# Key norms of a pair at once, spread by way of DRAM, in a hybrid RWKV-7 and dilated-attention layer

## The chip, the cores and the metric

One core of one Trainium2 chip. The metric is device time in microseconds of one execution; several executions give a median. The engines are TensorE (PE for products, PEld for its weight loads), VectorE (DVE), ScalarE (ACT), GpSimd (POOL) and SyncE (SP, which issues most DMAs).

## The reference

One layer of a decoder with two branches that run over the same projected input: RWKV-7 time mixing (8 heads of 64) and dilated attention (3 groups of 4 heads of 128). There are 1024 prompt tokens and 32 sample tokens (8 sequences of 4). The change lies in time mixing; what it computes there:

```python
h = x @ w_in                                   # (T, 9344): r | k | v | lora | gates | q | k | v | ...
zs_mixed = zs + mu_shift * (prev - zs)         # token shift of the first 1664 columns
w = -softplus(-(w0 + tanh(wd) @ w_w2)) - 0.5;  decay = exp(-exp(w))
a = sigmoid(a0 + ad @ w_a2)
kk = (k * k_k).reshape(B, T, R_HEADS, R_HD)
kk = kk / maximum(norm(kk, axis=-1), 1e-12)    # one norm for each token and head
k = k * (1.0 + (a - 1.0) * k_a)
# scan over tokens, per head:
#   sa = S @ (-kk_t);  S = S * w_t + sa (kk_t * a_t)^T + v_t k_t^T;  o_t = S @ r_t
```

then a group norm of o, a bonus term, a gate; the attention; and x <- LayerNorm(ALPHA x + W_out(g_r * (Y_r W_oa) + g_a * (Y_a W_ob))).

## The kernel before

The tokens run along the free dimension and the columns of the projections along the 128 partitions, so a column tile of 128 holds two heads of time mixing: a *pair*. A projection of one column tile (`project_steps`) is 72 products, in two halves of the contraction and three stretches of 352 tokens, into three banks of the tag `pj` (four in all). Its weights come in halves through `wraw` (two buffers) and are split into `whi` and `wlo` (three buffers each).

The time-mixing stage runs five streams against each other:

- `products`: for each of the four pairs the projections of k, r and v (`pair_tiles`, which keeps them shifted in tiles `m` of 1024 tokens, four buffers), and 24 projections that nothing in this stage needs soon (`fill`: gates), whose results go through tiles `zt` to DRAM. The projection of a pair's k may begin at once, those of r and v once `done["prep"] >= 2 * j`.
- `units`: eight preparations (`unit`), one for each pair j and half hf of 512 tokens. A unit squares the keys, sums the squares over each head's rows with a product against `bones` (lines 317 to 320), takes the inverse root in a chain of small DVE operations (`rsqrt`, lines 150 to 155), widens it to 64 columns a head (line 327), turns that back with four transposes (line 343), so that kkn, the normed keys, can be formed (line 345). Beside it go the low-rank products (line 301) and the decay. BK and KR are then multiplied in line 378, which gives AT. KR and what follows wait until the scan of the unit two places before is done.
- `inverses`: a triangular inverse on DVE for each unit. AT's blocks go by DRAM (Yd, then Y), lines 449 and 452 work on X, and X goes back by DRAM (Xd, line 456; AT from Xd, line 470), then T1 (line 471).
- `scans`: for each unit four rounds of small products (from line 476; lines 484 and 494 use T1), then eight hops, each two products (lines 535 and 541) with DVE and ACT between (lines 536, 537, 544).
- `norms`: group norm, gate, and the store of the branch's output.

`units` ends with `sample_rows`, which prepares the sample tokens' vectors and stores them to DRAM (`vd`).

The order of TensorE's instructions is written out by hand: `run_streams` keeps a clock of its own. Each generator yields a pair, the time that its products take and the delay after which it may go on (constants such as D_KR = 1.81, D_AT = 4.5, D_UP = 8.4 and D_ST, in us); between them pieces of `products` are put. A stream that yields None waits for a condition. The other engines' order comes from the scheduler below the kernel. All instructions of an engine, and all DMA issues of a queue, run in their order. After this stage come attention with its own projections, the two branch products, and the output product (line 1421).

The tag `g` has two PSUM banks (norm sums, low-rank products, transposes and others), `sc` two (scans).

Of the kernel before, what the change touches and what calls it, by code (L numbers as in the profile page):

```python
# [14 lines left out]
AF = mybir.ActivationFunctionType  # L15
ALU = mybir.AluOpType
AX = mybir.AxisListType

P = 128
D = 1024  # L20
KT = D // P
SEQ = 1024
NB = 8
NT = 4
NS = NB * NT
# [4 lines left out]

PIECE = 3
D_PN, D_KR, D_AT, D_G, D_W, D_INV, D_UP = 0.65, 1.81, 4.5, 0.2, 2.09, 1.3, 8.4
D_PM, D_HOP, D_ST, D_GN, D_IN, D_U0, D_MASK = 0.9, 1.25, 1.54, 12.6, 11.0, 1.2, 1.2
SMALL = 1.0
RS = 8
CDEC = math.exp(-0.5)
# [48 lines left out]
def tile_layer(ctx: ExitStack, tc: tile.TileContext, A: dict, O: list):  # L85
# [223 lines left out]
        return consume  # L309


    def unit(j, hf, Mr, Mk, Mv, st, out):
        sl = slice(512 * hf, 512 * hf + 512)
        t_ = lambda tag="t", n=6: mk(rp, [P, 512], tag, n)
        c2p = lambda a: a.rearrange("p (a b c) -> p a b c", a=4, b=2)
        sq = t_()
        S.activation(sq[:], Mk[:, sl], AF.Square, scale=prm[:, KK + j : KK + j + 1])
        pn = ps("g")
        for c2 in range(4):
            T.matmul(pn[:, 2 * c2 : 2 * c2 + 2], sq[:, c2 * P : (c2 + 1) * P], bones[:, 0:P:64], start=True, stop=True)  # L320
        yield (0.4, 0.6)
        nt = mk(rp, [P, 24], "nt", 1)
        n2, rn, tn = nt[:, 0:8], nt[:, 8:16], nt[:, 16:24]
        V.tensor_scalar(n2, pn[:, 0:8], 1e-24, None, ALU.max)
        rsqrt(rn, n2, tn)
        rb = t_()
        V.tensor_copy(rb.rearrange("p (a b) -> p a b", a=8), rn.unsqueeze(2).to_broadcast([P, 8, 64]))
        pw, pa = ps("g"), ps("g")
        lora(((pw[:], 0, j), (pa[:], 1, j)), sl)
        yield (1.3, D_PN)  # L330
# [6 lines left out]
        V.tensor_tensor_scan(lam[:], rmask, sg[:], 0.0, ALU.mult, ALU.add)  # L337
        Ei = t_()
        S.activation(Ei[:], lam[:], AF.Exp, scale=0.5 * CDEC)
        yield (0.0, D_KR)  # L340
        pn = ps("g")
        for c2 in range(4):
            T.transpose(pn[:, c2 * P : (c2 + 1) * P], rb[:, c2 * P : (c2 + 1) * P], ident)
        kkn = t_()
        V.scalar_tensor_tensor(kkn[:], Mk[:, sl], prm[:, KK + j : KK + j + 1], pn[:], ALU.mult, ALU.mult)
        bt = t_()
        V.scalar_tensor_tensor(bt[:], ta[:], 1.0, kkn[:], ALU.add, ALU.mult)
        f2 = t_()
# [3 lines left out]
        BK = mk(rp, [P, 4, 4, 64], "BK", 1)  # L352
        V.scalar_tensor_tensor(BK[:, :, 1:3, :], c2p(bt), 0.5, c2p(Ei), ALU.mult, ALU.mult)
        V.tensor_tensor(BK[:, :, 0:4:3, :], c2p(k2), c2p(Ei), ALU.mult)
        yield (0.45, 0.0)
        while done["scan"] < 2 * j + hf - 1:
            yield None
        E = mk(rp, [P, 8, 65], "E", 2)
        G.memset(E[:, :, 0:1], 1.0)
        S.activation(E[:, :, 1:65], lam.rearrange("p (a b) -> p a b", a=8), AF.Exp, scale=-0.5 * CDEC)  # L360
# [29 lines left out]
                )  # L390
            yield (0.9, D_MASK)
        masked.append((j, hf, AT))
        while done["norm"] < 2 * j + hf - 1:
            yield None
        bon = t_("bon", 2)
        pb = ps("g")
        T.matmul(pb[:], bones, rk[:], start=True, stop=True)
# [163 lines left out]
    def norm(j, hf, Ot, bon):  # L561
        sl = slice(512 * hf, 512 * hf + 512)
        t_ = lambda tag, n: mk(rp, [P, 512], tag, n)
        Og = Ot.rearrange("p a (b c) -> p (a b) c", b=2)
        m8 = mk(rp, [P, 8], "m8", 1)
        V.tensor_reduce(m8[:], Og, AX.X, ALU.add)
        V.tensor_scalar(m8[:], m8[:], 1.0 / 64.0, None, ALU.mult)
        V.tensor_tensor(Og, Og, m8.unsqueeze(2).to_broadcast([P, 8, 64]), ALU.subtract)
        sq = t_("sz", 2)
        S.activation(sq[:], Ot.rearrange("p a b -> p (a b)"), AF.Square)  # L570
        v8 = mk(rp, [P, 8], "v8", 1)
        V.tensor_reduce(v8[:], sq.rearrange("p (a b) -> p a b", a=8), AX.X, ALU.add)
        V.tensor_scalar(v8[:], v8[:], 1.0 / 64.0, GN_EPS, ALU.mult, ALU.add)
        nt = mk(rp, [P, 24], "nt", 1)
        r8 = nt[:, 0:8]
        rsqrt(r8, v8[:], nt[:, 8:16])
        V.tensor_tensor(Og, Og, r8.unsqueeze(2).to_broadcast([P, 8, 64]), ALU.mult)
        yield (0.0, D_GN)
        po = ps("g")
        for c2 in range(4):  # L580
            T.transpose(po[:, c2 * P : (c2 + 1) * P], Ot[:, c2, :], ident)
        y = Ot.rearrange("p a b -> p (a b)")
        S.activation(y, po[:], AF.Identity, scale=prm[:, LG + j : LG + j + 1], bias=prm[:, LB + j : LB + j + 1])
        V.tensor_tensor(y, y, bon[:], ALU.add)
        sz = t_("sz", 2)
        SP.dma_start(sz[:], zd[j, :, sl])
        V.tensor_tensor(y, y, sz[:], ALU.mult)
        SP.dma_start(yd[j, :, sl], y)
# [14 lines left out]
    pbc = lambda o: prm[:, o : o + 4].unsqueeze(2).to_broadcast([P, 4, NS])  # L603
    dbc = lambda o: der[:, o : o + 4].unsqueeze(2).to_broadcast([P, 4, NS])
    bns = mk(cpool, [P, 4, NS], "bns")
    vd = mk(dpool, [8, NS, 6, 64], "vd")


    def sample_rows():
        sgs, tas, nS, tS = (mk(rp, [P, 512], "t", 6)[:, 0:P].rearrange("p (a b) -> p a b", a=4) for _ in range(4))  # L610
        rS, kS_, vS_ = (sM[:, 4 * i : 4 * i + 4, :] for i in range(3))
        bs = [ps("g") for half in range(2)]
        for j in range(4):
            lora([(bs[half][:, NS * j : NS * j + NS], half, j) for half in range(2)], slice(SEQ, TOK))
        yield 0.6, D_G
        for b, dst, off in ((bs[0], sgs, HW0), (bs[1], tas, HA0)):
            for j in range(4):
                S.activation(dst[:, j, :], b[:, NS * j : NS * j + NS], AF.Tanh, scale=0.5, bias=der[:, off + j : off + j + 1])
        vec = mk(rp, [P, SEQ], "m", 4)[:, 0 : 24 * NS].rearrange("p (a b c) -> p a b c", a=6, b=4)

        V.tensor_scalar(sgs, sgs, 1.0, None, ALU.add)
        S.activation(vec[:, 0], sgs, AF.Exp, scale=-0.5 * CDEC)
        G.tensor_tensor(vec[:, 1], kS_, pbc(KK), ALU.mult)
        G.tensor_tensor(tS, vec[:, 1], vec[:, 1], ALU.mult)
        yield 0.0, 2.0
        b = ps("g")
        T.matmul(b[:, 0:P], bones, tS.rearrange("p a b -> p (a b)"), start=True, stop=True)
        nf = lambda a: a.rearrange("p a b -> p (a b)")
        V.tensor_scalar(nf(nS), b[:, 0:P], 1e-24, None, ALU.max)
        rS2 = mk(rp, [P, 512], "t", 6)  # L630
        rsqrt(rS2[:, 0:P], nf(nS), rS2[:, P : 2 * P])
        G.tensor_tensor(vec[:, 1], vec[:, 1], rS2[:, 0:P].rearrange("p (a b) -> p a b", a=4), ALU.mult)
        V.scalar_tensor_tensor(vec[:, 2], tas, 1.0, vec[:, 1], ALU.add, ALU.mult)
        V.tensor_scalar(vec[:, 2], vec[:, 2], 0.5, None, ALU.mult)
        G.tensor_tensor(vec[:, 3], tas, dbc(KAH), ALU.mult)
        G.tensor_tensor(vec[:, 3], vec[:, 3], dbc(KA2), ALU.add)
        G.tensor_tensor(vec[:, 3], vec[:, 3], kS_, ALU.mult)
        G.tensor_copy(vec[:, 4], rS)
        G.tensor_copy(vec[:, 5], vS_)
        G.tensor_tensor(tS, rS, vec[:, 3], ALU.mult)  # L640
        G.tensor_tensor(tS, tS, pbc(RK), ALU.mult)
        yield 0.2, 4.0
        b = ps("g")
        T.matmul(b[:, 0:P], bones, tS.rearrange("p a b -> p (a b)"), start=True, stop=True)
        V.tensor_tensor(bns[:], b[:, 0:P].rearrange("p (a b) -> p a b", a=4), vS_, ALU.mult)
        vt = mk(rp, [P, SEQ], "m", 4)[:, 0 : 6 * P].rearrange("p (a b) -> p a b", a=6)
        for h in range(2):
            yield 0.3, 1.0
            b = ps("g")
            for i in range(3):  # L650
                T.transpose(b[:, i * P : (i + 1) * P], vec[:, 3 * h + i].rearrange("p a b -> p (a b)"), ident)
            S.activation(vt[:, 3 * h : 3 * h + 3, :], b[:, 0 : 3 * P].rearrange("p (a b) -> p a b", a=3), AF.Copy)
        for hh in range(8):
            src = vt[NS * (hh // 2) : NS * (hh // 2) + NS, :, 64 * (hh % 2) : 64 * (hh % 2) + 64]
            SP.dma_start(vd[hh], src)

        yield 0.3, 1.0
        b = ps("g")
        T.transpose(b[0:117, 0:P], zl.rearrange("p a b -> p (a b)"), ident)
        zo = mk(rp, [P, P], "so", 1)  # L660
        V.tensor_copy(zo[0:117, :], b[0:117, 0:P])
        SP.dma_start(O[10][0, 0].rearrange("(a b) -> a b", b=P), zo[0:13, :])
        SP.dma_start(O[11][0].rearrange("s (a b) -> (s a) b", b=P), zo[13:117, :])
# [6 lines left out]
    def pair_tiles():  # L670
        for j in range(4):
# [2 lines left out]
                G.memset(t[:], 0.0)  # L674
            for c0, i, o in ((512, 1, 4), (0, 0, 0), (1024, 2, 8)):
                yield (lambda: True) if i == 1 else (lambda: done["prep"] >= 2 * j)
                M[i] = mk(rp, [P, SEQ], "m", 4)
                yield from project_steps(c0 + P * j, shifted(o + j, M[i]), PIECE)
            pairs[j] = M, st

    def products():
        pt = pair_tiles()
# [13 lines left out]
    def units():  # L696
        for u in range(8):
# [1 line left out]
            while j not in pairs:  # L699
                yield None  # L700
            M, st = pairs[j]
            yield from unit(j, hf, M[0], M[1], M[2], st, ready)
            done["unit"] += 1
        yield from sample_rows()

    def inverses():
# [760 lines left out]
```

## Time and profile before

| | us |
|---|---|
| median of 3 runs (lowest, highest) | 1369.14 (1366.88, 1371.59) |
| profiled execution, its time | 1371.35 |
| its span, first to last instruction | 1369.6 |
| busy: PE, PEld | 1331.2, 1241.9 |
| busy: DVE, ACT, POOL | 802.4, 469.4, 67.4 |
| mean granted TensorE clock | 0.993 |

All times in the rows are in us from the start of the span, unless marked ns. A row of a timeline has start, duration, engine, line, operation, what it writes and reads, how many instructions were merged (x), and in brackets how long the engine sat idle before it and what released it. A row of waits has who waited for whom, then total, times and longest. A row of a stretch has its length, then busy time and number of instructions of PE, PEld, DVE, ACT and POOL, the granted TensorE clock, the DMA engines' share and GB/s. A group's row has the count, then busy time and mean ns of one, then idle time before it. Rows of one line have minimum, median and maximum duration in ns, then first and last start. Matmuls are pipelined: a busy TensorE is not TensorE at its peak, and one instruction's duration is longer than the distance to the next. "PEq", "SPq" and the like are an engine's queue, which waits or issues.

### The profile page before, as it was taken

What the parts mean: (1) busy time and instruction counts of PE and PEld (TensorE: products, weight loads), DVE (VectorE), ACT (ScalarE), POOL (GpSimd) and SP (SyncE); (2) the same over time, 40 slices, a digit from 0 to 9 for tenths busy, and PEclk for the clock granted to TensorE, in tenths of its full rate; (3) what the DMA queues carried; (4) which work ended last, traced back from release to release, by engine and by line L of the source; (5) the groups of instructions that cost most, each with busy time, mean ns of one, the idle gap of its engine ahead of it and who ended that gap; (6) DMA issues with size and microseconds to landing.
All of it is one profiled execution on the core that took longest, in us unless ns stands there. A gap on an engine that the chain in (4) does not pass through costs nothing.

```text
span 1369.6 us, 25939 instructions
## 1 busy us (share of the span) xinstructions
PE 1331.2 (97%) x10097; PEld 1241.9 (91%) x10097; DVE 802.4 (59%) x2203; ACT 469.4 (34%) x1065; POOL 67.4 (5%) x82
## 2 busy tenths in 40 slices
PE   8999999999999999899999999999999998999997
PEld 7999899999998999899999999999999997899786
DVE  5467857685867757352554385437543744665565
ACT  5342434444444444332332323332332234132211
POOL 0000000000000000000000000000000000025100
PEclk9999999999999999899999999999999999999999
DMA  6123132313222232237555455555445666785221
GB/s 204 53 67 79 39 100 72 97 47 100 77 76 70 79 111 72 79 97 152 109 108 119 119 132 103 122 125 133 98 119 130 129 135 148 233 277 168 83 97 70
DMA packets 340271, 151.64 MB, mean 111 GB/s; under 512 B 188928, under 2 KB 329622, under 8 KB 339894
## 3 DMA queue, kind: packets, MB, share of 16 engines
q1 hardware_dynamic: 241270, 129.68, 34.4%
q10 hardware_dynamic: 98880, 20.32, 7.4%
q8 instruction: 79, 1.29, 0.4%
q14 instruction: 42, 0.34, 0.1%
HBM read 110.68 MB, written 38.97 MB: 109 GB/s over the span
## 4 chain that ended last, share of the span: by engine, by line
PE 81%; DVE 11%; DMA 4%; issue 2%; SPq 1%; ACT 1%; DVEq 0%; ACTq 0%
PE pj L173 59%; PE pj L1421 7%; PE o L975 2%; PE s L938 2%; DVE tm L449 2%; DVE X L452 2%; PE g L378 1%; PE t L958 1%; PE s L1057 1%; DMA cb<-cd 1%; DVE st L544 1%; PE sc L535 1%; DVE wlo L164 1%; PE sc L541 1%; PE g L552 1%
## 5 line engine op out<-in xcount | busy, mean ns | idle before, releaser
L173 PE MATMUL pj<-xhi,whi 128*128 128x352 f32 x1848 | 397.5, 336 | 4.6 <-ACT xhi L1288 3.0
L173 PE MATMUL pj<-xlo,whi 128*128 128x352 f32 x1848 | 384.2, 329 | 0.0
L173 PE MATMUL pj<-xhi,wlo 128*128 128x352 f32 x1848 | 383.6, 329 | 0.0
L173 PEld LDWEIGHTS pj<-xhi,whi 128*128 128x128 f32 x1848 | 304.9, 189 | 21.8 <-issue 11.4
L173 PEld LDWEIGHTS pj<-xlo,whi 128*128 128x128 f32 x1848 | 307.7, 190 | 2.7 <-issue 1.0
L173 PEld LDWEIGHTS pj<-xhi,wlo 128*128 128x128 f32 x1848 | 308.4, 190 | 1.8 <-issue 0.6
L164 DVE TENSOR_TENSOR wlo<-wraw,whi 128x512 fp32r<-128x512 f32 x162 | 113.1, 700 | 74.0 <-ACT whi L163 73.1
L163 ACT ACTIVATE whi<-wraw 128x512 fp32r<-128x512 f32 x162 | 100.5, 625 | 126.0 <-PE pj L173 80.8
L948 ACT ACTIVATE Sm<-Sm,nm 128x128 f32<-128x128 f32 (+1 forms) x96 | 42.4, 442 | 101.9 <-DVE nm L945 101.8
L449 DVE TENSOR_TENSOR tm<-Y,X 128x60 f32<-128x60 f32 (+24 forms) x248 | 52.7, 213 | 9.6 <-DMA Y<-Yd 3.7
L452 DVE TENSOR_TENSOR X<-X,tm 128x60 f32<-128x60 f32 (+24 forms) x248 | 52.3, 211 | 6.2
L940 DVE CUSTOM_DVE_ANT_0 Sm<-s,cst 128x128 f32<-128x128 f32 (+1 forms) x96 | 29.2, 346 | 40.6 <-PE s L938 40.0
L1421 PE MATMUL pj<-wl,mh 128*128 128x512 f32 (+1 forms) x136 | 52.0, 382 | 0.0
L544 DVE SCALAR_TENSOR_TENSOR st<-sc,E,SD 64x64 f32<-64x64 f32 x128 | 36.1, 282 | 22.8 <-PE sc L541 21.2
L533 ACT ACTIVATE SD<-st,E 128x128 f32<-128x128 f32 x64 | 25.6, 400 | 57.8 <-DVE st L544 57.7
L801 POOL TENSOR_TENSOR kvp<-vv,kv 128x512 f32<-128x512 f32 x16 | 19.7, 1234 | 498.0 <-DVE Ss L809 387.5
L975 PE MATMUL o<-PT,Vt 128*128 128x128 f32 x280 | 38.8, 276 | 0.8 <-ACT PT L962 0.8
L863 ACT ACTIVATE k<-pj 128x352 f32<-128x352 f32 (+1 forms) x36 | 16.2, 454 | 67.0 <-PE pj L173 62.7
L938 PE MATMUL s<-k,q 128*128 128x128 f32 (+1 forms) x192 | 37.7, 325 | 0.8 <-DVE ml L940 0.8
L975 PEld LDWEIGHTS o<-PT,Vt 128*128 128x128 f32 x280 | 36.4, 191 | 1.5 <-ACT PT L962 1.1
L536 DVE TENSOR_TENSOR W<-sc,R 64x128 f32<-64x128 f32 x64 | 18.4, 288 | 31.8 <-PE sc L535 30.7
L537 ACT ACTIVATE Ot<-sc 64x128 f32<-64x128 f32 x64 | 17.3, 270 | 57.5 <-DVE W L536 57.4
(320 smaller groups left out, 1706.7 us busy)
## 6 DMA issues: line engine op xcount, KB each, us to landing
wraw<-in_w_in_dram SPq DMA_DIRECT2D x146, 256.0 KB
gd<-zt SPq DMA_DIRECT2D x48, 176.0 KB
gt<-gd SPq DMA_DIRECT2D x48, 176.0 KB
vs<-bt ACTq DMA_DIRECT2D x48, 128.0 KB
kc<-in_cache_kv_g_dram SPq DMA_DIRECT2D x48, 128.0 KB
Vt<-vs ACTq DMA_DIRECT2D x12, 512.0 KB
cb<-cd SPq DMA_DIRECT2D x12, 512.0 KB
zd<-zt SPq DMA_DIRECT2D x24, 176.0 KB
```

What stands on the lines that cost most here:

```text
L163: S.activation(hi[:], raw[:], AF.Copy)
L164: V.tensor_tensor(lo[:], raw[:], hi.bitcast(F32)[:], ALU.subtract)
L173: T.matmul(out, w[wi][:, n % 4, :], x[:, n % 4, :], start=first and n == 0, stop=last and n == 11)
L449: V.tensor_tensor(tm, Y[:, r : r + 1, r + 1 : 32].to_broadcast([P, m, n]), X[:, 0:m, r : r + 1].to_broadcast([P, m, n]), ALU.mult)
L452: V.tensor_tensor(X[:, 0:m, r + 1 : 32], X[:, 0:m, r + 1 : 32], tm, ALU.subtract)
L533: S.activation(SD[:], S0[:], AF.Copy, scale=E[:, c, 64:65])
L544: V.scalar_tensor_tensor(S1[d, d], pS[d, d], E[d, c, 64:65], SD[d, d], ALU.mult, ALU.add)
L938: T.matmul(r, qT[:, i * P : (i + 1) * P], kT[:, keys[i][0] * P : keys[i][0] * P + n], start=True, stop=True)
L940: V.tensor_tensor_reduce(out=Sm[:, i, 0:n], in0=r, in1=m3 if g == 2 else m12[:, 256 - n : 256], scale=1.0, scalar=NEG, op0=ALU.add, op1=AL ...
L948: S.activation(Sm[:, i, 0:n], Sm[:, i, 0:n], AF.Exp, scale=SCALE, bias=nm[:, x : x + 1], accum_out=ml[:, g, 1, i : i + 1])
L975: T.matmul(po[:, (i % 4) * P : (i % 4 + 1) * P], st["Vt"][:, kb_, :], PT[:, n * P : (n + 1) * P], start=m == 0, stop=m == len(keys[i]) - 1,)
L1421: T.matmul(pb[:], a[:, k], wk, start=x == 0, stop=x == len(prods) - 1)
```

## The change

The norms of a pair are formed once, in its first unit (hf = 0), for both halves: two squares, eight products into 16 columns of one bank, one chain of small operations on 16 columns. The 128x16 result is stored to a DRAM tile `nd` [4, 2, 1024] in the order (pair, head of the pair, token). Each unit then loads its half, each head's row broadcast to the head's 64 partitions, into the tile `rb`, in the layout of the keys. The widening copy and the four transposes go. The delay ahead of kkn is doubled in first units, and the yield behind BK goes.

`pair_tiles` hands the pair over when its k is projected, and `unit` takes r and v out of the dictionary M where it needs them, waiting until they are there. `sample_rows` waits for seven scans, and stores `vd` with two DMAs in place of eight. D_ST is 1.65 in place of 1.54.

```diff
-D_PM, D_HOP, D_ST, D_GN, D_IN, D_U0, D_MASK = 0.9, 1.25, 1.54, 12.6, 11.0, 1.2, 1.2
+D_PM, D_HOP, D_ST, D_GN, D_IN, D_U0, D_MASK = 0.9, 1.25, 1.65, 12.6, 11.0, 1.2, 1.2
...
-    def unit(j, hf, Mr, Mk, Mv, st, out):
+    def unit(j, hf, M, st, out):
+        Mk = M[1]
...
-        sq = t_()
-        S.activation(sq[:], Mk[:, sl], AF.Square, scale=prm[:, KK + j : KK + j + 1])
-        pn = ps("g")
-        for c2 in range(4):
-            T.matmul(pn[:, 2 * c2 : 2 * c2 + 2], sq[:, c2 * P : (c2 + 1) * P], bones[:, 0:P:64], start=True, stop=True)
-        yield (0.4, 0.6)
-        nt = mk(rp, [P, 24], "nt", 1)
-        n2, rn, tn = nt[:, 0:8], nt[:, 8:16], nt[:, 16:24]
-        V.tensor_scalar(n2, pn[:, 0:8], 1e-24, None, ALU.max)
-        rsqrt(rn, n2, tn)
+
+        if hf == 0:
+            pn = ps("g")
+            for x in range(2):
+                sq = t_()
+                S.activation(sq[:], Mk[:, 512 * x : 512 * x + 512], AF.Square, scale=prm[:, KK + j : KK + j + 1])
+                for c2 in range(4):
+                    n = 4 * x + c2
+                    T.matmul(pn[:, n:16:8], sq[:, c2 * P : (c2 + 1) * P], bones[:, 0:P:64], start=True, stop=True)
+                yield (0.8, 0.6)
+            nt = mk(rp, [P, 48], "nt", 1)
+            n2, rn, tn = nt[:, 0:16], nt[:, 16:32], nt[:, 32:48]
+            V.tensor_scalar(n2, pn[:, 0:16], 1e-24, None, ALU.max)
+            rsqrt(rn, n2, tn)
+            SP.dma_start(nd[j].rearrange("e (c p) -> p (e c)", p=P), rn)
         rb = t_()
-        V.tensor_copy(rb.rearrange("p (a b) -> p a b", a=8), rn.unsqueeze(2).to_broadcast([P, 8, 64]))
+        for e in range(2):
+            SP.dma_start(rb[64 * e : 64 * e + 64, :], nd[j, e : e + 1, sl].to_broadcast([64, 512]))
         pw, pa = ps("g"), ps("g")
...
-        yield (0.0, D_KR)
-        pn = ps("g")
-        for c2 in range(4):
-            T.transpose(pn[:, c2 * P : (c2 + 1) * P], rb[:, c2 * P : (c2 + 1) * P], ident)
+        yield (0.0, D_KR if hf else 2.0 * D_KR)
         kkn = t_()
-        V.scalar_tensor_tensor(kkn[:], Mk[:, sl], prm[:, KK + j : KK + j + 1], pn[:], ALU.mult, ALU.mult)
+        V.scalar_tensor_tensor(kkn[:], Mk[:, sl], prm[:, KK + j : KK + j + 1], rb[:], ALU.mult, ALU.mult)
...
-        yield (0.45, 0.0)
-        while done["scan"] < 2 * j + hf - 1:
+        while done["scan"] < 2 * j + hf - 1 or 0 not in M:
             yield None
+        Mr = M[0]
...
-        while done["norm"] < 2 * j + hf - 1:
+        while done["norm"] < 2 * j + hf - 1 or 2 not in M:
             yield None
+        Mv = M[2]
...
-        for hh in range(8):
-            src = vt[NS * (hh // 2) : NS * (hh // 2) + NS, :, 64 * (hh % 2) : 64 * (hh % 2) + 64]
-            SP.dma_start(vd[hh], src)
+        for e in range(2):
+            SP.dma_start(vd.rearrange("(j e) s i c -> e j s i c", e=2)[e], vt[:, :, 64 * e : 64 * e + 64])
...
-                M[i] = mk(rp, [P, SEQ], "m", 4)
-                yield from project_steps(c0 + P * j, shifted(o + j, M[i]), PIECE)
-            pairs[j] = M, st
+                m = mk(rp, [P, SEQ], "m", 4)
+                yield from project_steps(c0 + P * j, shifted(o + j, m), PIECE)
+                M[i] = m
+                pairs[j] = M, st
...
-            yield from unit(j, hf, M[0], M[1], M[2], st, ready)
+            yield from unit(j, hf, M, st, ready)
             done["unit"] += 1
+        while done["scan"] < 7:
+            yield None
         yield from sample_rows()
```

The chain of small operations in the group norm takes its tile `nt` in the new size as well.

More of the change, by code (lines that the diff above doesn't have):

```diff
@@ L573, in norm @@
         V.tensor_scalar(v8[:], v8[:], 1.0 / 64.0, GN_EPS, ALU.mult, ALU.add)
-        nt = mk(rp, [P, 24], "nt", 1)
+        nt = mk(rp, [P, 48], "nt", 1)
         r8 = nt[:, 0:8]
@@ L605, in tile_layer @@
     bns = mk(cpool, [P, 4, NS], "bns")
+    nd = mk(dpool, [4, 2, SEQ], "nd")
     vd = mk(dpool, [8, NS, 6, 64], "vd")
```

## The prediction

> **What bounds the kernel now.** I read the page first, then the busy time by stretch, then TensorE's waits inside the stage that the change touches, and last the one place where these stand out. From the page: busy time, the slices, and the shares of the chain that ended last.
>
> ```profile
> PE 1331.2 (97%) x10097; PEld 1241.9 (91%) x10097; DVE 802.4 (59%) x2203; ACT 469.4 (34%) x1065; POOL 67.4 (5%) x82
> ...
> PE   8999999999999999899999999999999998999997
> ...
> PEclk9999999999999999899999999999999999999999
> ...
> PE 81%; DVE 11%; DMA 4%; issue 2%; SPq 1%; ACT 1%; DVEq 0%; ACTq 0%
> ```
>
> TensorE is busy 97% of the span and the chain runs over it. So time falls where TensorE gets fewer instructions, or where it stands. The recurrent stage, to about 619 us, has one slice with a lower clock. Its stretches of 50 us and its waits:
>
> ```profile
> 500.00:550.00 50.00, 47.91 (x478) 44.93 (x477) 29.73 (x112) 22.97 (x56) 2.69 (x6) 1.00 0.30 86
> 550.00:600.00 50.00, 46.23 (x376) 44.51 (x375) 19.59 (x52) 16.54 (x38) 0.00 (x0) 0.90 0.27 81
> ```
> ```profile
> PE sc L535 <- DVE st L544: 8.0, 10, 1.2
> PE sc L484 <- DVE T L471: 3.8, 2, 3.6
> PE g L301 <- DVE nt L324: 1.3, 2, 1.1
> ```
>
> The first row is the hop of the scan, ten waits of at most 1.2 us. The second is one stop at one place. TensorE there, then the stretches with the granted clock (the column after POOL's):
>
> ```profile
> 557.37 0.22 PE L484 MATMUL sc<-T,AT 32*32 32x32 f32 x2 [3.61 <-DVE T L471]
> ```
> ```profile
> 553.40:557.40 4.00, 0.39 (x4) 0.13 (x3) 3.56 (x15) 2.00 (x4) 0.00 (x0) 1.00 0.55 125
> 557.40:558.00 0.60, 0.44 (x12) 0.33 (x14) 0.29 (x1) 0.00 (x0) 0.00 (x0) 0.77 0.99 309
> 558.00:568.00 10.00, 10.00 (x117) 8.98 (x112) 0.00 (x0) 2.16 (x6) 0.00 (x0) 0.50 0.15 43
> ```
>
> A stop of 3.6 us, then 10 us at half clock, "busy" all the while: 3.8 + 10.0 x 0.5 + 0.6 x 0.23 = 8.9 us lost. Why is T (line 471) late? The queue SP and DVE of that unit, the eighth, and then the first unit for comparison:
>
> ```profile
> 536.71 0.17 DVE L452 TENSOR_TENSOR X<-X,tm 128x8 f32<-128x8 f32 x1
> 536.91 1.21 SPq L456 DMA_DIRECT2D Xd<-X  x2
> 538.85 5.08 SPq L655 DMA_DIRECT2D vd<-m  x8
> 545.75 1.36 SPq L456 DMA_DIRECT2D Xd<-X  x2
> 552.49 1.83 SPq L470 DMA_DIRECT2D AT<-Xd  x4
> 556.79 0.90 DVE L471 STREAM_TRANSPOSE T<-AT 32x256 f32<-32x256 f32 x2
> ```
> ```profile
> 123.61 0.17 DVE L452 TENSOR_TENSOR X<-X,tm 128x8 f32<-128x8 f32 x1
> 131.05 0.44 DVE L471 STREAM_TRANSPOSE T<-AT 32x256 f32<-32x256 f32 x1 [0.94 <-DMA AT<-Xd]
> ```
>
> The inverse is ready at 536.9; the first unit then needs 7.3 us to T, the eighth 19.9. Between its first two stores and its last two stand the eight stores of sample_rows (5.1 us of issue) and the waits around them.
>
> **The change, part by part.** *Transposes.* Each unit loses four 128x128 transposes (line 343). Norm products stay at eight a pair.
>
> ```profile
> L343 PE MATMUL g<-ident,t x32: 270/272/273, 70.7 to 467.9; 128*128 128x128 f32 x32
> ```
> ```profile
> 70.68 0.60 PE L343 MATMUL g<-ident,t 128*128 128x128 f32 x4
> ```
>
> Four take 0.60 us, of which the last one's 0.27 is latency: (0.60 - 0.27) / 3 = 0.11 us apart. 32 x 0.11 = 3.5 us of TensorE's time, where it has other work queued: **-3.5 us**.
>
> *DVE.* Eight spread copies (line 327) and half of the eight chains of ten small operations (lines 324 and 151 to 155) go:
>
> ```profile
> L347 DVE SCALAR_TENSOR_TENSOR t<-t,t 128x512 f32<-128x512 f32 x8 | 5.5, 684 | 0.1
> ...
> L327 DVE COPY t<-nt 128x512 f32<-128x512 f32 x8 | 3.4, 425 | 0.1
> ...
> L154 DVE TENSOR_TENSOR nt<-nt 128x8 f32<-128x8 f32 x48 | 7.8, 163 | 1.0
> ```
>
> 3.4 us, and 4 x 11 operations some 0.2 us apart, about 9 us. DVE is not the bound, so 0; at best it takes some of the 8.0 us of hop waits. Sixteen columns in place of eight, and kkn reading SBUF in place of PSUM, are 0. The wait of line 301 on the norm's bank has four chances in place of eight; it is 1.3 us in all now, so 0.
>
> *The detour by DRAM.* Per pair one store nd of 128 x 16 single values (each value lies apart in DRAM, 2048 pieces) and four broadcast loads rb: 20 DMAs on SP, all told. The trace has no such store; nearest are the stores N of 512 single values, and the pair cd/cb, a small store with a broadcast load behind it:
>
> ```profile
> N<-ml SPq DMA_DIRECT2D x16, 2.0 KB
> ```
> ```profile
> 912.24 2.87 DMA cd<-nE
> 915.56 7.26 DMA cb<-cd
> ...
> 1121.59 4.22 DMA N<-ml
> ```
>
> Lower bound of the trip: the 7.3 us from X to T above, four stores and four loads. Upper: 4.2 + 7.3 = 11.5 us, though cb is 512 KB and rb 128 KB. I take 7.5, near the lower, since rb resembles the AT and Y loads in size. [...]
>
> What waits for it? kkn on DVE, then BK and KR, then the products of line 378. The planner allows from the norm products to kkn 0.6 + 1.3 + 0.65 + 2 x 1.81 = 6.2 us; real are 2.3 (small operations) + 7.5 = 9.8. For pairs 1 to 3 line 378 comes long after; the tightest case now:
>
> ```profile
> 414.81 0.49 PE L301 MATMUL g<-lorh,lhi 64*128 64x512 f32 x1
> ...
> 434.30 1.16 PE L378 MATMUL g<-KR,BK 64*128 64x128 f32 x16
> ```
>
> 19 us cover the trip, and the unit may now start before r and v are projected. The pair 0 has no such cover. Its keys are in at 41.3, and now its line 378 comes at 76:
>
> ```profile
> 40.77 0.55 DVE L237 SCALAR_TENSOR_TENSOR m<-pj,prm,m 128x319 f32<-128x319 f32 x1 [1.20 <-ACT m L236]
> ```
> ```profile
> 76.37 1.16 PE L378 MATMUL g<-KR,BK 64*128 64x128 f32 x16
> ```
>
> After the change: norm products done near 43, r projected by 53 (the planner's 72 x 0.148 = 10.7 us of products, and 2 of the unit's own), plus D_AT 4.5: the planner puts line 378 near 58. The data: 43 + 2.3 + 7.5 = 53, then five DVE operations of 0.7 (as line 347) and KR's two, with r's shift between: 59. So a stop of **+1 us**; with 11.5 us for the trip, 5.
>
> DVE is in order: if its order has kkn too early it stands, and hop and shift operations behind it with it; SP stands at the rb issue until nd has landed, with weights and stores behind it. Now, with the trips Y and T of the same kind:
>
> ```profile
> DVE tm L449 <- DMA Y<-Yd: 3.7, 2, 3.2
> ...
> DVE T L471 <- DMA AT<-Xd: 1.7, 4, 0.9
> ```
>
> Sixteen trips cost DVE 5.4 us in six waits, so three more pairs about 1 to 2: **+1.5 us**; bounds 0 and 3 x 3.2 = 10. SP's block of some 4 us is covered by three weight buffers and four projection banks.
>
> *sample_rows* moves behind the seventh scan, beside the eighth, and stores with two DMAs in place of eight. Then nothing of it stands between Xd's stores. With a trip of 7 to 9 us T is there by 546, over 10 us ahead of line 484. **-8.9 us.** Its DVE operations share DVE with a scan, as they do now (with the seventh); POOL, which takes its products, is busy 67 us of the whole span, and no work of a unit is left behind it there.
>
> *Starting at the keys, and D_ST 1.54 to 1.65.* Both move the chain of scans, not TensorE's work:
>
> ```profile
> L535 PE MATMUL sc<-st,KR x128: 270/274/378, 147.1 to 601.6; 128*128 128x128 f32 x128
> ```
> ```profile
> L199 ACT ACTIVATE zt<-pj x24: 439/464/467, 89.6 to 619.2; 128x352 f32<-128x352 f32 x24
> ```
>
> The chain ends near 605, the independent projections at 619. It starts 18 us sooner (76 to 58), gets at most 64 x 0.11 = 7 us longer and loses the 8.9: end near 585. Projections still cover it: 0. Without that cover each us of chain would count.
>
> Sum: -3.5 - 8.9 + 1 + 1.5 = -9.9. The profiled execution took 1371.35 us (span 1369.6), 2.2 over the median of 1369.14; the difference is put on the median: **1359 us**.
>
> **Rivals.** *(B) The stop stays or moves.* The new order of TensorE sets every wait anew; a late T elsewhere costs the same 8.9, and only the transposes remain: 1369.1 - 3.5 + 1 = 1366.6. For: SP gets 20 DMAs more. Against: seven units of eight reach T with time to spare.
> *(C) Slower: DVE stands at kkn.* If DVE's order follows the planner, it stands 9.8 - 6.2 = 3.6 us in each of pairs 1 to 3, while a scan runs. TensorE stops as long, and 3.6 us is just the stop that halved the clock above: 3 x (3.6 + 5.1) = 26 us against a gain of 12.4: 1383. Without the clock it is 11 us, even. It decides once two such stops are long enough. Against: the Y and T waits above, and 19 us ahead of line 378.
> *(D) One long stop at pair 0.* A trip of 10 us or more gives a stop of 3.6 us and 5.1 of half clock: 1359.2 + 2.6 + 5.1 = 1367. [...]
> *(E) The change does less than it says*: the early start brings nothing. That is my own sum already.
>
> **How the numbers follow.** My case 0.65 (1351 to 1364: all of the hop waits' 8 us gone at the low end, detour terms doubled and more at the high), B 0.12, D 0.10, C and other new stops 0.13. 0.3% is 4.1 us, about what a measurement here can tell from none. Faster 0.65; B and D fall within, 0.22; slower 0.13. The range to 1369 takes in B and D, leaving C and some 0.05 below: 1351 to 1369.
>
> **What would show it.** Line 343 gone, and 3.5 us of TensorE with it. No wait of line 484 over 1 us, a clock of 1.00 from 50 us to 619, T 7 to 9 us behind X in the eighth unit. First products of line 378 near 58, waiting about 1 us. DVE's waits on rb under 1 us a pair. The last line 535 well ahead of the last zt. I am wrong if DVE or TensorE shows stops over 3 us tied to rb, or the clock falls anywhere in the stage, or projections run out before the scans.

## The result, and the profile after

| | before | after |
|---|---|---|
| median of 4 runs each, us (lowest, highest) | 1368.53 (1366.88, 1371.59) | 1401.14 (1398.56, 1402.35) |
| profiled execution, its span, us | 1371.35, 1369.6 | 1398.56, 1396.8 |
| mean granted TensorE clock | 0.993 | 0.984 |

The ratio is 1.0233 (95% interval 1.0215 to 1.0252): 32 us slower, where 10 us faster were forecast. From the page of the kernel after, the same rows as were shown of before:

```profile
PE 1331.9 (95%) x10065; PEld 1240.9 (89%) x10065; DVE 800.9 (57%) x2151; ACT 470.4 (34%) x1065; POOL 66.4 (5%) x82
...
PE   8896999979996999999999999999999999899997
...
PEclk9998999999998999999999999999999999999999
```

TensorE has its 32 instructions less, and the same busy time over a span that is 27 us longer. So it stands more. The holes lie in the first third of the slices, in the time-mixing stage. The stage's last zt shows how much of the loss is there:

```profile
L199 ACT ACTIVATE zt<-pj x24: 444/464/466, 164.5 to 647.8; 128x352 f32<-128x352 f32 x24
```

It ended at 619.2 and ends at 647.8: 28.6 us later, which is all of the profiled difference of 27.2. Stretches of the stage (columns as before: length, then PE, PEld, DVE, ACT and POOL, the clock, the DMA share, GB/s):

```profile
50.00:100.00 50.00, 44.50 (x311) 41.40 (x311) 28.02 (x81) 17.35 (x33) 0.00 (x0) 0.93 0.19 51
100.00:150.00 50.00, 39.39 (x373) 35.57 (x373) 33.12 (x123) 16.03 (x32) 0.00 (x0) 0.90 0.24 59
400.00:450.00 50.00, 38.43 (x284) 36.49 (x283) 34.75 (x131) 16.61 (x37) 1.10 (x3) 0.90 0.18 47
550.00:600.00 50.00, 49.91 (x466) 47.92 (x465) 23.41 (x70) 20.86 (x52) 2.63 (x6) 1.00 0.34 97
```

The last row is the old stop's stretch, now without a hole and at full clock. The first three hold four of the five new long stops; the fifth ends at 302.2. The waits of the stage, for TensorE, then DVE, then the queue SP:

```profile
PE sc L540 <- DVE st L549: 23.5, 13, 10.4
PE sc L489 <- DVE T L476: 10.5, 2, 6.4
PE pj L173 <- DVE lst L241: 5.1, 1, 5.1
```
```profile
DVE t L349 <- DMA t<-nd: 26.0, 3, 10.0
```
```profile
SPq L334 <- DMA nd<-nt: 39.5, 4, 10.6
```

Read from below. SP waits four times, 10.6 us at most, for the store nd to land before it may issue the loads rb. DVE then stands 26.0 us at kkn (line 349 writes a tile of the tag t), in three of the four pairs, 10.0 us at most. TensorE waits for things that have nothing to do with the norms: st, T, lst. What these have in common is DVE's order, here at the first pair, the second and the fourth:

```profile
60.14 0.75 DVE L349 SCALAR_TENSOR_TENSOR t<-m,prm,t 128x512 f32<-128x512 f32 x1 [10.04 <-DMA t<-nd]
60.81 0.58 DVE L237 SCALAR_TENSOR_TENSOR m<-pj,prm,m 128x351 f32<-128x351 f32 x1
61.30 0.15 DVE L241 COPY lst<-pj 128x1 f32<-128x1 f32 x1
...
132.66 0.43 DVE L476 STREAM_TRANSPOSE T<-AT 32x256 f32<-32x256 f32 x1 [7.19 <-DMA AT<-Xd]
...
429.31 0.75 DVE L349 SCALAR_TENSOR_TENSOR t<-m,prm,t 128x512 f32<-128x512 f32 x1 [7.77 <-DMA t<-nd]
...
430.95 0.27 DVE L549 SCALAR_TENSOR_TENSOR st<-sc,E,SD 64x64 f32<-64x64 f32 x1
```
```profile
61.60 1.51 PE L173 MATMUL pj<-xhi,whi 128*128 128x352 f32 x4 [5.14 <-DVE lst L241]
...
137.51 0.69 PE L489 MATMUL sc<-T,AT 32*32 32x32 f32 x18 [4.05 <-DVE T L476]
...
302.21 0.77 PE L540 MATMUL sc<-st,KR 128*128 128x128 f32 x2 [8.30 <-DVE st L549]
...
433.48 0.76 PE L540 MATMUL sc<-st,KR 128*128 128x128 f32 x2 [10.42 <-DVE st L549]
```

In the first pair the shift of the running projection (lines 237 and 241) stands behind kkn, its PSUM bank is not freed, and the projection stops. In the third and fourth the hop's st stands behind kkn, and the running scan stops. In the second T is late, in both its halves. The queue SP there:

```profile
121.48 0.38 SPq L331 DMA_DIRECT2D nd<-nt  x1
122.04 1.74 SPq L475 DMA_DIRECT2D AT<-Xd  x3
132.04 1.14 SPq L334 DMA_DIRECT2D t<-nd  x2
133.22 0.59 SPq L475 DMA_DIRECT2D AT<-Xd  x1
```

Each half of T needs two of the four loads of AT. Those of the first half were issued at 122, right behind nd. By the stretches of the trace the DMA engines moved nothing from 129 to 132 us (0 GB/s), yet DVE got this half only at 132.66, 0.6 us behind the landing of nd, which let rb go at 132.04. So the slow store also held up the loads issued behind it; in e1 below the same three loads stand behind a store that lands in 1.4 us, and DVE doesn't wait for them. That is the stop of 6.43 us; it was over at 133.15, before the fourth load was issued behind rb at 133.22. The second half stands behind kkn on DVE and starts at 137.03 without waiting for a DMA: the stop of 4.05 us. It comes of the new order and not of the landing, as e1 below shows.

The account: the five long stops are 5.14 + 6.43 + 4.05 + 8.30 + 10.42 = 34.3 us. Half clock comes with them, as in this stretch:

```profile
427.00:439.00 12.00, 5.52 (x22) 5.55 (x23) 7.39 (x22) 1.51 (x4) 0.69 (x1) 0.57 0.21 66
```

It sets in at 59.3, 131.0, 298.3 and 428.0, while TensorE still stands, 2.9 to 4.9 us behind the start of a stop, and lasts to 66.1, 141.2, 305.1 and 438.2, that is 4.5, 3.7, 2.9 and 4.7 us beyond the ends of the stops at 61.6, 137.5, 302.2 and 433.5: 15.8 us at half speed lose 7.9. Against that stand the old stop (8.9) and shorter stops. From 50 us to the last zt TensorE was idle for 14.6 us before and 42.3 after; without the long stops (3.8 and 34.3) that is 10.8 and 8.0, so 2.8 less. 34.3 + 7.9 - 8.9 - 2.8 = 30.5, with 28.6 measured. The sum is 1.9 us too long; whether these are a part of the 3.5 us of the transposes it can't tell.

### The profile page after: what moved, and what is told of

Its sections match the earlier page's. It is cut to its first block, busy times and chain, and to the rows that moved or that the text cites. A ratio compares the mean times of both kernels' runs of the same rounds, so it can differ in the third digit from the quotient of the medians.

```text
span 1396.8 us, 25857 instructions
## 1 busy us (share of the span) xinstructions
PE 1331.9 (95%) x10065; PEld 1240.9 (89%) x10065; DVE 800.9 (57%) x2151; ACT 470.4 (34%) x1065; POOL 66.4 (5%) x82
## 4 chain that ended last, share of the span: by engine, by line
PE 51%; DMA 3%; DVE 3%; SPq 1%; issue 1%; POOL 0%; ACT 0%; DVEq 0%; POOLq 0%
PE pj L173 37%; PE pj L1429 6%; PE o L983 2%; PE s L946 2%; DMA cb<-cd 1%; PE t L966 1%; PE s L1065 1%; DVE o L1229 1%; DMA cd<-nE 1%; SPq L1125 1%; DMA kc<-in_cache_kv_g_dram 0%; PE so L1364 0%; DVE o L1232 0%; PE s L1084 0%; PE t L1134 0%
## 5 line engine op out<-in xcount | busy, mean ns | idle before, releaser
L173 PE MATMUL pj<-xhi,wlo 128*128 128x352 f32 x1848 | 388.3, 331 | 0.0
L540 PEld LDWEIGHTS sc<-st,KR 128*128 128x128 f32 x128 | 21.8, 192 | 32.2 <-issue 17.4
L540 PE MATMUL sc<-st,KR 128*128 128x128 f32 x128 | 26.9, 292 | 23.6 <-DVE st L549 23.5
L871 ACT ACTIVATE k<-pj 128x352 f32<-128x352 f32 (+1 forms) x36 | 16.1, 454 | 64.4 <-PE pj L173 60.3
```

The costliest lines, as they stand in the source:

```text
L173: T.matmul(out, w[wi][:, n % 4, :], x[:, n % 4, :], start=first and n == 0, stop=last and n == 11)
L540: T.matmul(pr[:, 0:P], KR[:, c2, 2 * p : 2 * p + 2, :], S0[:], start=True, stop=True)
```

## The experiments

The theory ahead of the first runs was that the loss is the slow landing of nd, by way of DVE's and SP's order; rivals were the yields that set DVE's order, and the other parts of the change (early start, moved rows, D_ST). Each batch ran with runs of the kernel before on its own chip, whose medians were 1370.2 (e1 to e4), 1368.9 (e5, e7, e8, p8), 1370.2 (e6, e9, p16, p4_half) and 1370.5 us (e11, p4_apart); ratios are against these.

### Which part loses the time

**e1_store64.** The store with another shape: 128 pieces of 64 bytes in place of 2048 of 4. The norms then belong to other tokens; all else stays.

```diff
-            SP.dma_start(nd[j].rearrange("e (c p) -> p (e c)", p=P), rn)
+            SP.dma_start(nd[j].rearrange("e (q x) -> (e q) x", x=16), rn)
```

> The changed kernel, with the store of nd in the order in which the values lie (128 pieces of 64 bytes in place of 2048 single values); the loads rb get norms of other tokens. The orders of TensorE, DVE and ACT stay as they are. Theory 1 (the store of single values to DRAM lands 10.6 us after its issue, and DVE, in order, stands at kkn and SP at rb): landing in 2.5 to 4 us as cd's 64-byte pieces (2.87 us), DVE's waits on nd's loads under 6 us in all in place of 26, no stop of TensorE over 4 us, 1362 to 1372 us. Theory 2 (the new order of TensorE, with units that start at the keys, makes the stops whatever the store does): the stops stay where they are, 1393 to 1402 us.

Measured: 1366.46 us, ratio 0.9965 (0.9947 to 0.9983). The first trip on SP, and DVE's whole wait in the stage:

```profile
45.86 0.34 SPq L331 DMA_DIRECT2D nd<-nt  x1
47.29 1.10 SPq L334 DMA_DIRECT2D t<-nd  x2
```
```profile
DVE t L349 <- DMA t<-nd: 0.8, 1, 0.8
```

From nd's issue to rb's: 1.4 us, where it was 10.6. DVE's wait falls from 26.0 to 0.8 us, and 2.7% of the time goes with it. So the loss is the landing of this store, in its shape; the same bytes to the same place do not cost it. One of the five stops stays: T's second half still stands behind kkn on DVE, and TensorE waits 3.5 us for it at 122.7.

**e7_detour_only.** The kernel before with the detour alone: no early start, sample_rows and its eight stores as before, D_ST 1.54 (line 347 is its kkn).

```diff
+            SP.dma_start(nd[j].rearrange("e (c p) -> p (e c)", p=P), rn)
...
-        V.tensor_copy(rb.rearrange("p (a b) -> p a b", a=8), rn.unsqueeze(2).to_broadcast([P, 8, 64]))
+        for e in range(2):
+            SP.dma_start(rb[64 * e : 64 * e + 64, :], nd[j, e : e + 1, sl].to_broadcast([64, 512]))
```

> The kernel before with nothing but the detour (norms of a pair at once, single values, rb loads, 2 x D_KR): units start when k, r and v are in, sample_rows and D_ST as before. If the detour alone makes the stops: landing 10.6 us, DVE stands 5 to 10 us at three or four pairs, each with its half clock, and the old stop of 8.9 us stays too: 1390 to 1410 us. If the early start is a condition for them: 1366 to 1376 us.

Measured: 1395.3 us, 1.0186 (1.0163 to 1.0209).

```profile
DVE t L347 <- DMA t<-nd: 26.7, 4, 9.6
```
```profile
PE sc L542 <- DVE W L537: 17.3, 6, 8.1
PE g L379 <- DVE BK L356: 8.4, 1, 8.4
PE pj L173 <- DVE lst L241: 7.0, 1, 7.0
```

DVE's standing makes four stops of TensorE, of 7.0 to 8.4 us, elsewhere; it also stands 8.3 us in one wait for the loads of AT ahead of T (line 472), where the kernel before has 0.9 at most. The early start is not needed for the loss: without it the first pair's products of AT wait 8.4 us.

**e5_late_kkn.** The planner is told that kkn comes late; D_KR is four times as long in first units.

```diff
-        yield (0.0, D_KR if hf else 2.0 * D_KR)
+        yield (0.0, D_KR if hf else 8.0 * D_KR)
```

> The changed kernel, single values and all, with 8 x D_KR (14.5 us) in place of 2 x D_KR ahead of kkn in first units, so that kkn and what follows are issued later. The store still lands in 10.6 us and SP still stands at rb. If DVE's standing at kkn makes the stops: DVE's waits on nd's loads fall from 26 us to under 6, the stops at 56, 294 and 423 us go, and what is left is SP's (the one near 126 us); 1368 to 1380 us. If SP's standing (late weights, late T) makes them: all stay, 1390 us and more.

Measured: 1396.58 us, 1.0198 (1.0175 to 1.022).

```profile
DVE t L349 <- DMA t<-nd: 26.1, 4, 11.2
```

The stand is the same 26 us. A longer allowance for the trip doesn't mend it: at the first pair the same operations stand ahead of kkn on DVE as before (the last is line 164, at 49.3), and DVE waits 11.2 us there. What sets kkn's place on DVE isn't shown.

**e6_pool_queue.** Both DMAs of the detour on GpSimd's queue, so that SP has no wait in it.

```diff
-            SP.dma_start(nd[j].rearrange("e (c p) -> p (e c)", p=P), rn)
+            G.dma_start(nd[j].rearrange("e (c p) -> p (e c)", p=P), rn)
...
-            SP.dma_start(rb[64 * e : 64 * e + 64, :], nd[j, e : e + 1, sl].to_broadcast([64, 512]))
+            G.dma_start(rb[64 * e : 64 * e + 64, :], nd[j, e : e + 1, sl].to_broadcast([64, 512]))
```

> The changed kernel with nd's store and rb's loads issued by GpSimd in place of SP; single values as they were. SP is free of the wait, DVE isn't. If DVE's standing at kkn makes most of the loss: its waits on nd's loads stay above 20 us, the stops at 56, 294 and 423 us stay, and only the one near 126 us (T's load queued behind rb on SP) goes: 1385 to 1398 us. If SP's standing makes most: 1366 to 1378 us.

Measured: 1402.79 us, 1.0236 (1.0212 to 1.026). The landing of nd, then DVE's wait and TensorE's for T:

```profile
DMA to landing us min/median/max: 11.8/12.3/13.5
```
```profile
DVE t L349 <- DMA t<-nd: 36.9, 4, 11.7
PE sc L489 <- DVE T L476: 13.7, 2, 12.9
```

The landing is as slow on the other queue. The stop near 130 was to go with SP's block. T's first half is mended: AT's loads stay on SP's queue, where nd no longer stands; DVE waits 1.2 us for them and TensorE 0.8 for T. The second half stands behind kkn on DVE, 12.9 us in one wait. So this pair has two ways to a stop: the loads behind the store, and DVE's order.

### What makes the store slow

**p8_store, p16_store, p4_half, p4_apart.** Only the pieces of nd's store change; the norms reach other tokens, or none in p4_apart. p8: 1024 pieces of 8 bytes; p16: 512 of 16; p4_half: the first head as 1024 single values, the second as 128 pieces of 32 bytes; p4_apart: 2048 single values, each 64 bytes from the next.

```diff
-            SP.dma_start(nd[j].rearrange("e (c p) -> p (e c)", p=P), rn)
# p8 (x=2), p16 (x=4)
+            SP.dma_start(nd[j].rearrange("e (y q x) -> q (e y) x", q=P, x=2), rn.rearrange("p (y x) -> p y x", x=2))
# p4_half
+            SP.dma_start(nd[j, 0].rearrange("(c p) -> p c", p=P), rn[:, 0:8])
+            SP.dma_start(nd[j, 1].rearrange("(p c) -> p c", p=P), rn[:, 8:16])
# p4_apart; nd is 16 times as long and zeroed once
+            SP.dma_start(nd[j].rearrange("e (c p z) -> p (e c) z", p=P, z=16)[:, :, 0:1], rn.unsqueeze(2))
```

> The changed kernel with nd stored in 1024 pieces of 8 bytes in place of 2048 of 4 (the loads get norms of other tokens); orders of TensorE, DVE and ACT unchanged. Measures the landing of the store against the number of pieces: 2048 pieces took 10.6 us, 128 pieces 1.4. If landing goes with the number of pieces: 1.4 + 9.2 x (1024 - 128) / 1920 = 5.7 us. If it goes with single values alone (each a part of a word or line): 1.5 to 3 us. If with any piece under some size: near 10 us.

> The changed kernel with nd stored in 512 pieces of 16 bytes (the loads get norms of other tokens). Landings so far: 2048 pieces of 4 bytes 10.6 us, 1024 of 8 bytes 4.5, 128 of 64 bytes 1.4. If landing goes with the number of pieces: 2.5 to 3 us. If pieces of 8 bytes and more are all alike and only the count of bytes matters: 4 us and more.

> The changed kernel with nd stored by two DMAs, one for each head of the pair: the first in 1024 single values, the second in 128 pieces of 32 bytes (the second head's loads get norms of other tokens). If the number of pieces sets the landing: as 1024 pieces of 8 bytes, 4 to 6 us. If single values are dear in themselves and the 8 bytes cheap: 6 us and more, with the first head's loads the late ones.

> The changed kernel with each of the 2048 single values of nd 64 bytes from the next (the DRAM tile is 16 times as large and zeroed at the start; the loads read its first part, mostly zeros, so the keys' norms are left out). Landing so far: 2048 single values side by side 10.6 us, 1024 of them 9.3 to 11.8, 1024 pieces of 8 bytes 4.5, 512 of 16 bytes 2.6, 128 of 64 bytes 1.4. If what counts is how many pieces share a stretch of 64 bytes: under 3 us, and the stops over 4 us go (1362 to 1372 us). If the width of a piece counts by itself: 9 us and more, and the stops stay (1390 to 1405 us).

Single runs: 1378.99, 1366.42, 1403.89, 1370.04 us. From SP's timelines, the first nd and the first rb behind it, in p4_half and then in p4_apart; the table has the starts of the same two rows for all:

```profile
45.87 0.37 SPq L331 DMA_DIRECT2D nd<-nt  x1
46.29 0.57 SPq L332 DMA_DIRECT2D nd<-nt  x1
55.66 1.10 SPq L335 DMA_DIRECT2D t<-nd  x2
```
```profile
46.16 0.37 SPq L331 DMA_DIRECT2D nd<-nt  x1
50.25 1.10 SPq L334 DMA_DIRECT2D t<-nd  x2
```

| pieces of the store | nd and rb issued at, us | between, us |
|---|---|---|
| 2048 of 4 bytes, side by side in DRAM (after) | 45.97, 56.70 | 10.7 |
| 1024 of 4 bytes side by side, and 128 of 32 (p4_half) | 45.87, 55.66 | 9.8 |
| 2048 of 4 bytes, 64 bytes apart (p4_apart) | 46.16, 50.25 | 4.1 |
| 1024 of 8 bytes (p8) | 46.02, 50.48 | 4.5 |
| 512 of 16 bytes (p16) | 45.83, 48.47 | 2.6 |
| 128 of 64 bytes (e1) | 45.86, 47.29 | 1.4 |

Half as many single values side by side cost nearly the same; twice as many of them apart cost less than half. The 4.5 us of p8 are less than the 5.7 that the number of pieces would give, the 9.8 of p4_half more than the 4 to 6. So neither the number of pieces nor their width alone explains the 10.7. The two stores of 2048 values differ in how they lie in DRAM: side by side, 16 in each 64 bytes, 10.7 us; 64 bytes apart, 4.1. That 64 is the width that counts isn't shown: it is the only distance tried, and with it the values were spread over 16 times as much DRAM. p4_apart came out between its two expectations in the landing (4.1 us, not under 3 nor over 9), and with the first of them in the time.

### Where the expected gain is

**e4_rows_moved.** The kernel before with only sample_rows moved and its stores merged.

```diff
-        for hh in range(8):
-            src = vt[NS * (hh // 2) : NS * (hh // 2) + NS, :, 64 * (hh % 2) : 64 * (hh % 2) + 64]
-            SP.dma_start(vd[hh], src)
+        for e in range(2):
+            SP.dma_start(vd.rearrange("(j e) s i c -> e j s i c", e=2)[e], vt[:, :, 64 * e : 64 * e + 64])
...
+        while done["scan"] < 7:
+            yield None
```

> The kernel before, with sample_rows behind the seventh scan and its store in two DMAs, nothing else. If the stop of 3.8 us and the 10.2 us of half clock came from sample_rows standing between the stores of the eighth inverse: both go, T is ready 7 to 9 us behind X, 1359.6 us (1357 to 1363). If they came from the inverse being last and late anyway: the stop stays within 1 us of its size, 1366 to 1371 us.

Measured: 1364.58 us, 0.9947 (0.9928 to 0.9967), 7.3 us by the ratio. X, T and line 484 of the eighth unit, then the stretch where the half clock was, then the last zt:

```profile
536.26 0.16 DVE L452 TENSOR_TENSOR X<-X,tm 128x8 f32<-128x8 f32 x1
546.88 0.43 DVE L471 STREAM_TRANSPOSE T<-AT 32x256 f32<-32x256 f32 x1
560.25 0.69 PE L484 MATMUL sc<-T,AT 32*32 32x32 f32 x32
```
```profile
545.00:570.00 25.00, 25.00 (x306) 23.29 (x305) 15.84 (x44) 11.86 (x30) 3.25 (x6) 1.00 0.27 82
```
```profile
L199 ACT ACTIVATE zt<-pj x24: 445/466/468, 89.3 to 610.5; 128x352 f32<-128x352 f32 x24
```

T is there 13 us ahead of line 484, TensorE stands nowhere in these 25 us, and the stage ends 8.7 us sooner. This part alone beats both kernels.

**e3_norms_by_pe and e9_d_st.** The kernel after with the norms of before (copy, transposes, no detour); the early start, the moved rows and D_ST stay. e9 is e3 with D_ST at its old value.

```diff
-D_PM, D_HOP, D_ST, D_GN, D_IN, D_U0, D_MASK = 0.9, 1.25, 1.65, 12.6, 11.0, 1.2, 1.2
+D_PM, D_HOP, D_ST, D_GN, D_IN, D_U0, D_MASK = 0.9, 1.25, 1.54, 12.6, 11.0, 1.2, 1.2
```

> The changed kernel with the norms of each unit as before (per half, copy and four transposes, no DRAM), and the rest of the change left in: start at the keys, sample_rows behind the seventh scan with two stores, D_ST 1.65. Theory 1: no stop over 2 us in the stage, the old stop before line 484 of the eighth unit gone with its half clock, 1368.5 - 8.9 = 1359.6 us, 1356 to 1364. Theory 2: the stops of the changed kernel stay, 1390 us and more.

> e3_norms_by_pe (the change without the detour) with D_ST back at 1.54, so e4_rows_moved plus the early start alone. e4 took 1364.6 us, e3 1368.9. If the early start costs the 4 us (T's transpose of the first unit queued behind the next pair's preparation on DVE, near 119 us): that stop of 2 to 4 us with its half clock stays, 1367 to 1371 us. If D_ST costs them: no such stop, 1362 to 1366 us.

Measured: e3 1368.9 us, 0.999 (0.9976 to 1.0004); e9 1364.07 us, 0.9955 (0.9942 to 0.9967). In e3 the gain of e4 is gone without any detour. The first place where the profiled executions of e3 and e9 part, T1's products of the first unit and the 11 us behind them, e3 first:

```profile
121.48 1.06 PE L488 MATMUL sc<-T,AT 32*32 32x32 f32 x30 [2.15 <-DVE T L475]
```
```profile
121.00:132.00 11.00, 10.52 (x118) 9.39 (x118) 9.63 (x41) 3.29 (x9) 0.00 (x0) 0.53 0.09 25
```
```profile
121.27 0.69 PE L488 MATMUL sc<-T,AT 32*32 32x32 f32 x30 [2.15 <-DVE T L475]
```
```profile
121.00:132.00 11.00, 10.73 (x171) 9.85 (x172) 9.93 (x43) 4.48 (x12) 0.00 (x0) 1.00 0.10 27
```

The same stop of 2.15 us is followed by half clock in e3 (118 products in 11 us) and by none in e9 (171). 11 us at a clock of 0.53 lose 5.2 us, and the 0.35% between the ratios are 4.8. But D_ST did not cause this spell: up to 196 us TensorE and DVE run the same instructions in the same order in both kernels. Nor is the clock all of the difference: at the same mean clock of 0.995, two runs of e3 took 1367.0 and 1367.7 us, five of e9 1363.1 to 1364.2. Some 3 us are left; the two ran on different chips, and what makes them is open. The early start brings nothing: e9, which has it, is no faster than e4, which has not.

**e2_row_store, e11_rows_d_st, e8_rows_and_moved.** The detour with a store in 16 rows of 512 bytes: one transpose a pair turns the sums, and the small operations run on 16 partitions. e2 is the kernel after with that; e11 is e2 with D_ST 1.54; e8 is e4 with that detour and without the early start.

```diff
-            n2, rn, tn = nt[:, 0:16], nt[:, 16:32], nt[:, 32:48]
-            V.tensor_scalar(n2, pn[:, 0:16], 1e-24, None, ALU.max)
+            V.tensor_scalar(nt[:, 0:16], pn[:, 0:16], 1e-24, None, ALU.max)
+            yield (0.0, 0.6)
+            pt = ps("g")
+            T.transpose(pt[0:16, 0:P], nt[:, 0:16], ident)
...
+            V.tensor_copy(n2, pt[0:16, 0:P])
             rsqrt(rn, n2, tn)
-            SP.dma_start(nd[j].rearrange("e (c p) -> p (e c)", p=P), rn)
+            SP.dma_start(nd[j].rearrange("e (c p) -> (e c) p", p=P), rn)
```

> The changed kernel, with the 128x16 sums turned by one transpose a pair and the chain of small operations on 16x128, so that nd is stored in 16 rows of 512 bytes, in token order. Theory 1: four transposes (0.4 us) more for TensorE, landing under 4 us, no stop over 4 us, 1358 to 1368 us. Theory 2: 1390 us and more. A third possibility: the longer way to nd (a PSUM copy and 128 columns in each of ten small operations, some 1.5 us) leaves DVE standing 2 to 4 us at two or three pairs, 1368 to 1378 us.

> e2_row_store (the whole change, with nd in 512-byte rows) with D_ST at 1.54. D_ST was worth 4.8 us between e3 and e9, and the transposes are 3.5 us less the 0.4 of the new ones. If both hold here: e9's 1364.1 - 3 = 1361 us (1358 to 1363.5). If the detour's waits eat the transposes as they did between e3 and e2: 1364 to 1366. If D_ST's gain belongs to the norms by transposes alone: 1368 to 1371.

> The kernel before with the two parts that paid: norms of a pair at once with sums turned by one transpose and nd stored in 512-byte rows; sample_rows behind the seventh scan with two stores. Units start when k, r and v are in, D_ST 1.54. Theory 1: e4's 1364.6 less 28 transposes at 0.11 us: 1361.5 us (1358 to 1364), landing under 2 us, no stop over 2 us. Rival: DVE, with wider small operations and rb to wait for, stands 2 to 3 us at some pairs, each enough to halve the clock for some us: 1364 to 1370.

Measured: e2 1369.6 us, 0.9989 (0.9973 to 1.0004); e11 1367.93, 0.9984 (0.997 to 0.9998); e8 1368.29, 0.9987 (0.9971 to 1.0003). All three missed the gain expected of them. The slow landing is mended (nd to rb 1.9 us in e2) and 28 of 32 transposes are gone, but by the ratios e11 lies 4.0 us above e9 and e8 5.5 us above e4, the kernels with all transposes. TensorE's waits for the hop, in e9, e11 and e8:

```profile
PE sc L539 <- DVE st L548: 7.8, 7, 1.8
```
```profile
PE sc L546 <- DVE st L555: 9.5, 13, 2.0
PE sc L495 <- DVE T L482: 3.9, 3, 2.0
```
```profile
PE sc L542 <- DVE st L551: 12.5, 15, 2.6
```

Many small waits take the place of the transposes: from 50 us on, all waits of TensorE in the stage are 16.1 us in e11 and 12.5 in e9, and 16.9 in e8 against 8.7 in e4. In e8 the scans end at 616, later than the projections (614), so the last hops have no projections beside them. Why these waits grow isn't settled; no run took the order of DVE as it is and left out only the transposes.

## Why the prediction was wrong, by its steps

- *The detour's price is the step that failed.* It gave the trip 7.5 us, near the 7.3 from X to T, and 11.5 at most, with nd's landing taken from the row of N, 4.2 us for 512 single values. Measured: 10.6 to 11.1 us from nd's issue to rb's and 3.4 more to kkn (56.7 to 60.1), 14 in all. Neither row was of the same kind: Xd is stored in pieces of 128 bytes, and N is no store to DRAM but a copy from one tile of SBUF to another. Neither said anything of single values side by side in DRAM. On GpSimd's queue too this store took 11.8 to 13.5 us (e6).
- *What waits for it.* "19 us cover the trip" counted TensorE's distance to line 378. DVE stood at kkn and ran nothing else meanwhile (10.04 us at the first pair), with st, T and lst behind it. The warning stood in the prediction, at a price of 1.5 us with 10 as its bound; DVE stood 26.0 us. The bound came from the waits for Y and T, 3.2 us at most, on shorter trips (7.3 us from X to T).
- *Pair 0*: a stop of 1 us was forecast ahead of line 378, 5 with the long trip. It was 5.1 us, at the projection instead, and line 378 (now 382) began at 67.8, not 58.
- *SP's block "is covered"*: the cover was counted for weights. No long stop came of the block itself, but AT's loads behind nd on the queue landed only with it, and that was a stop of 6.4 us. No term of the prediction had it.
- *The second half of T behind kkn*, a stop of 4.05 us: it comes from DVE's new order and was in no term either. It is 3.5 us in e1 and 2.15 in e3 and e9.
- *Rival C was the mechanism*, DVE standing at kkn while a scan runs, with a chance of 0.13 and a stand of 3.6 us a pair; real stops were 4 to 10 us. Its condition, that DVE's order follows the planner, isn't borne out at the first pair by e5. Rival D, the long stop with half clock at pair 0, came too. Both were right in kind, and undersized by the same landing.
- *The stop at the eighth unit, -8.9*: right. T is 8.9 us behind X (551.7 to 560.6) in the kernel after, and e4 shows the gain alone: 7.3 us by the ratio, 8.7 in the stage.
- *Transposes, -3.5*: not shown. e1, without any, is 3.4 us under e3, but their intervals touch; e2, e8 and e11 show none of it.
- *Early start, 0*: right (e9 against e4). *D_ST, 0*: wrong by 4.8 us in e3 against e9, of which some 3 us remain at the same clock; why is open.
- *The clock*: the five stops of 4 to 10 us brought four spells of half clock, as the stop of 3.6 us in the kernel before had one. But of their 34 us 18.2 lie within the long stops, so the four cost 7.9 us, not the 5.1 each that C counted.

## What to carry to other kernels

Price a small store to DRAM by the shape of its pieces, from a row with the same kind of destination: the same 8 KB landed in 10.7 us as 2048 values side by side, in 1.4 as 128 pieces of 64 bytes. Turning the data on chip first made the pieces longer (in e2 that mended the landing, 1.9 us, and brought no gain over the kernel before). A load's cover is counted on the engine that consumes it, in its own order: name what stands behind the consumer there. Here that was st, T and lst behind kkn on DVE, and four of TensorE's five long stops, 27.9 us. Name also what is issued behind a slow store on its queue (here AT's loads, and a stop of 6.4 us). Of a change in several parts run each alone: here one part of four (sample_rows moved) held the whole gain.

## What the runs showed of the hardware

DMA engines were hardly busy for most of the time that this store was waited for. Two stretches of the kernel after, from nd's issue on:

```profile
45.90:49.00 3.10, 3.10 (x21) 3.10 (x20) 1.69 (x3) 1.53 (x3) 0.00 (x0) 1.00 0.30 3
49.00:56.00 7.00, 7.00 (x46) 7.00 (x45) 0.69 (x1) 4.56 (x9) 0.00 (x0) 1.00 0.02 1
```

The engines' share is 0.30 in the first 3.1 us and 0.02 in the 7 us after, yet rb, which waits for the landing, is issued only at 56.70. So most of the wait lies behind the recorded packets; what fills it isn't shown. The store took 10.7 us for 8 KB here on SP's queue and 11.8 to 13.5 on GpSimd's (e6); in 64-byte pieces the same 8 KB landed in 1.4 us (e1), and as single values 64 bytes apart in 4.1 (p4_apart). Why values side by side take longer isn't shown either; whether a store of as many values to SBUF does the same wasn't tried.

Loads issued behind this store were held up with it. With AT's loads right behind nd, T started 0.6 us after nd's landing in the kernel after (132.04 and 132.66), and DVE stood 7.2 us for them; in e1, with the same three loads behind a landing of 1.4 us, it did not stand for them, and in e6, with nd on GpSimd's queue, 1.2 us. In e5 and e7 its longest waits for AT's loads are 7.1 and 8.3 us.

A stop of 2.15 us was followed by half clock in the profiled execution of one kernel (e3, 0.53 from 121 to 132 us) and not in that of another (e9, 1.00), at the same place within 0.2 us and with the same instructions ahead of it. So the length of this stop alone doesn't tell whether the clock falls. What else counts stays open.
